# Strassen's seven products for the v, u and g products of a gMLP layer

## The chip, the core and the metric

The kernel runs on one core of one Trainium2 chip. The metric is the device time of one execution in microseconds (us). TensorE (PE) multiplies, VectorE (DVE), ScalarE (ACT) and GpSimd (POOL) do the rest, and SyncE (SP) and GpSimd issue the transfers between DRAM and the core's on-chip memory.

## The reference, cut to what matters

One sequence of 2048 tokens with 1024 features goes through one gMLP layer (A) and one attention layer (B), in float32. The change is in layer A's input product.

```python
def gmlp_mixer(h, w_in, ln_g, ln_b, ws, bs, w_out):
    z = h @ w_in                          # 1024 -> 3 * 2048
    u, v, g = jnp.split(z, 3, axis=-1)
    v = layer_norm(v, ln_g, ln_b)
    ...
    sv = jnp.einsum('gts,bcsgd->bctgd', wsm, v) + bs.T[:, :, None]   # per chunk of 128 tokens, 16 groups
    y = u * sv * jax.nn.silu(g)
    return y @ w_out

h = x + gmlp_mixer(rms_norm(x, a_norm_g), ...)
# then swa_mixer (attention in a window of 128 tokens) and a last rms_norm
```

## The kernel before

The tokens are worked in four blocks of 512 (`TB`), first all four through layer A, then all four through layer B. To keep float32's precision, every dense operand is split into a high and a low part (`split`: ACT casts the high part, DVE or POOL subtracts it for the low part), and each product is three matrix products (`mm3`): high by high, high by low, low by high.

A block of layer A has three stages. `vphase` makes v with tokens on partitions: 4 column blocks of 512, and for each of them 4 weight slabs, with 24 products of 512 columns a slab. Then come 16 column groups j of 128: `proj` makes u and then g for each, one slab and 24 products of 512 columns each, and `gate(j)` follows a product later: four small products with the spatial weights on TensorE, two steps on DVE, a multiply on POOL (L381), and a `split` on ACT and DVE. Last, `outproj_a` makes the output product with 16 slabs and adds x.

Weights come as slabs of 128x1024 (512 KB). `fetch` loads one from the SP queue into one of two raw buffers (`w_raw`), and `split` turns it into one of four buffers `w` (high and low part); `weights` hands out the next and keeps three fetched or under way. The raw buffer is free again after DVE's subtraction, and the `w` buffer after the last product that reads it.

Other work is put between the products by a count of half slabs: `half` advances the count, and `after(n, f)` calls f some halves later. In this way come the norm of x (`sumsq_step`, `rnorm`, `xn_step`), the next block's sums of squares, and `prescale`, which multiplies layer B's weights by a gain on POOL, splits them and stores them in DRAM, in 18 jobs. The framework's scheduler then sets the final order on each engine's queue, and each engine works its queue strictly in that order. On-chip tiles of 128x512 (`slot`) come from one pool of 39; there are eight PSUM banks (`bank`).

Of the kernel before, what the change touches and what calls it, by code (L numbers as in the profile page):

```python
# [18 lines left out]
P = 128  # L19
# [7 lines left out]
NJ = AW // P  # L27
NQ = 4
# [9 lines left out]
GEN_BUFS = 39  # L38
# [6 lines left out]
GATE_ENG = 'V'  # L45
FIRST_W = (0, 2, 5)
PIECES = "k00 k01 q00 q01 g00 q10 q11 g01 q20 q21 g10 q30 q31 g11 g20 g21 g30 g31".split()
# [9 lines left out]
def trunk(ctx: ExitStack, tc: tile.TileContext, xT, wv, wug, wao, wkv, wqg, wbo, wsT, bs, gains, lngb,  # L57
# [6 lines left out]
    xpool = ctx.enter_context(tc.tile_pool(name="xpool", bufs=8))  # L64
    gen = ctx.enter_context(tc.tile_pool(name="gen", bufs=GEN_BUFS))
    sm = ctx.enter_context(tc.tile_pool(name="sm", bufs=6))
    psum = ctx.enter_context(tc.tile_pool(name="psum", bufs=8, space=bass.MemoryType.PSUM))
# [5 lines left out]
    wkvD, wqgD = wbD[:2], wbD[2:]  # L73

    chain = [None]

    def load(dst, src):
        """A load from the sync queue; while chain is set, in the order of the program."""
        if chain[0] is None:
            nc.sync.dma_start(dst, src)  # L80
            return
        with tc.issue_after(chain[0]):
            chain[0] = nc.sync.dma_start(dst, src).ins
# [103 lines left out]
    def by_token(mean, n):  # L187
        """(mean + eps)^-1/2 of n * 128 tokens, from mean on every partition to [P, n] by token."""
# [10 lines left out]
    def rnorm(acc, done, wait=RN1, wait2=RN2, on_r4=None):  # L199
        """Calls done(r) with r on every partition, some half pieces later; on_r4 gets it by token."""  # L200
# [42 lines left out]

    def hn_steps(b, hh, hl):
        """The steps that make hn of a block, one per feature tile."""
        box = []

        def step(k):
            if not box:
                r = slot()  # L250
                nc.sync.dma_start(r, rD[b])
                box.append(r)
            raw = slot()
            nc.sync.dma_start(raw, hD[b][k])
            V.tensor_tensor(raw, raw, box[0], ALU.mult)
            h = xpool.tile([P, TB], F32R, name="x_hi")
            l = xpool.tile([P, TB], F32R, name="x_lo")
            split(h, l, raw)
            hh.append(h)
            hl.append(l)  # L260
# [3 lines left out]
    # ================= layer A =================  # L264
    with ExitStack() as actx:
        ac = actx.enter_context(tc.tile_pool(name="ac", bufs=1))
        pre = actx.enter_context(tc.tile_pool(name="pre", bufs=1))
        wraw[0] = pre

        ws_sb = ac.tile([P, NJ, P], F32, name="ws_sb")  # L270
        lngb_sb = ac.tile([P, 2, NJ], F32, name="lngb_sb")
        ln_g, ln_b = lngb_sb[:, 0, :], lngb_sb[:, 1, :]
        cb = ac.tile([P, NJ, P], F32, name="cb")

        def load_consts():
            load(ws_sb, wsT)
            G.affine_select(out=ws_sb, in_=ws_sb, pattern=[[0, NJ], [1, P]], base=0, channel_multiplier=-1,
                            compare_op=ALU.is_ge, fill=0.0)
            load(lngb_sb, lngb)
            load(cb.rearrange("p j t -> p (j t)"), bs.partition_broadcast(P))  # L280
            chain[0] = None

# [15 lines left out]
        def xn_step(k, xr, r, xh, xl):  # L298
            V.scalar_tensor_tensor(xr, xr, a_g[:, k:k + 1], r, ALU.mult, ALU.mult)
            h = xpool.tile([P, TB], F32R, name="x_hi")  # L300
            l = xpool.tile([P, TB], F32R, name="x_lo")
            split(h, l, xr)
            xh.append(h)
            xl.append(l)

        def make_cb():
            for q in range(4):
                ps = bank()
                PE.matmul(ps, ones, ws_sb[:, 4 * q:4 * q + 4, :], start=True, stop=True)
                for i in range(4):  # L310
                    j = 4 * q + i
                    V.scalar_tensor_tensor(cb[:, j, :], ps[:, i * P:(i + 1) * P], ln_b[:, j:j + 1], cb[:, j, :],
                                           ALU.mult, ALU.add)
# [12 lines left out]
        def prescale_job(src, dst, g, nk):  # L326
            w = pre.tile([P, 1024], F32, name="pw")
# [3 lines left out]
            hl = pre.tile([P, 2048], F32R, name="phl")  # L331
# [3 lines left out]
        def vphase(xh, xl, r4=None):  # L335
            vt = [[None] * 4 for _ in range(TT)]
            st = [sm.tile([P, 4, 6], F32, name="bst", bufs=8) for _ in range(TT)]
            for cbk in range(4):
# [12 lines left out]
                for t in range(TT):  # L351
                    v = slot()
                    if r4 is None:
                        A.copy(v, pss[t])
                    else:
                        A.activation(v, pss[t], AF.Copy, scale=r4[0][:, t:t + 1])
                    V.bn_stats(st[t][:, cbk, :], v)
                    vt[t][cbk] = v
            for t in range(TT):
# [5 lines left out]
                G.tensor_tensor(rs, ve, neghalf, ALU.pow)  # L365
                for cbk in range(4):
# [3 lines left out]
        def gate(j, vt, psu, psg, yh, yl):  # L370
            sg = slot()
            A.activation(sg, psg, AF.Silu)
            psm = bank()
            for t in range(TT):
                PE.matmul(psm[:, t * P:(t + 1) * P], vt[t][j // 4][:, (j % 4) * P:(j % 4 + 1) * P], ws_sb[:, j, :],  # L375
                          start=True, stop=True)
            sv = slot()
            V.scalar_tensor_tensor(sv.rearrange("p (c t) -> p c t", c=TT), psm.rearrange("p (c t) -> p c t", c=TT),
                                   ln_g[:, j:j + 1], cb[:, j, None, :].broadcast_to([P, TT, P]), ALU.mult, ALU.add)
            V.tensor_tensor(sv, psu, sv, ALU.mult)  # L380
            last[0] = G.tensor_tensor(sv, sv, sg, ALU.mult).ins  # L381
            h, l = slot(F32R), slot(F32R)
            split(h, l, sv)
            yh.append(h)
            yl.append(l)
# [21 lines left out]
        xh, xl, r4 = [], [], []  # L407
# [9 lines left out]
        def first_xn(r):  # L417
            for k in range(KD):
                after(2 * k, lambda k=k: xn_step(k, raws[k], r, xh, xl))
# [11 lines left out]
        after(18, make_cb)  # L431
        for b in range(NB):
            vt = vphase(xh, xl) if b else vphase(fh, fl, r4)
            yh, yl = [], []
            pend = None
            for j in range(NJ):
                psu = proj(xh, xl)
                if pend:
                    gate(*pend)
                psg = proj(xh, xl)  # L440
                pend = (j, vt, psu, psg, yh, yl)
                if j % 2 == 1:
                    prescale()
                if b + 1 < NB and j == 6:
                    for k, f in enumerate(stat_steps(b + 1, got.append)):
                        after(2 * k, f)
            gate(*pend)
            if b + 1 < NB:
                xh, xl = [], []
                r = got.pop()  # L450
                for k in range(KD):
                    after(2 * k + 1, lambda k=k, b=b, r=r, xh=xh, xl=xl: xn_step(k, load_x(b + 1, k), r, xh, xl))
# [8 lines left out]
    # ================= layer B =================  # L461
# [16 lines left out]
    def rope(src, nh, t0, nt, tab):  # L478
        """src [P, nt, nh, 64] rotated, as [P, nt * nh * 64] of a new slot."""
# [12 lines left out]
    def natural(ps, t2, t, w2, hh, hl):  # L492
        """ps[:, t2, :] = hn[t].T @ W for 256 columns."""
# [73 lines left out]
    def g_piece(i, sg, hh, hl):  # L567
        A.copy(sg[:, i, :], proj(hh, hl))
# [306 lines left out]
```

## Time and profile before

| | us |
|---|---|
| median of 3 runs | 2268.8 (2268.7 to 2269.88) |
| span of the profiled execution | 2266.6 |
| TensorE busy, by the profile's model | 2239.9 |
| DVE, ACT, POOL busy | 1240.9, 889.2, 619.3 |

The profile describes one execution, from its first to its last instruction. Of that execution only the span is given, 2.2 us under the median of the three runs. Line numbers (L113) are those of the kernel before. In groups, a number after x is a count, and "idle before" names what ended the wait. In the rows for one tile, three numbers with strokes are the shortest, the median and the longest duration in ns.

### The profile page before, as it was taken

Reading aid. Unit: us, or ns where it says so; the run is one execution under the profiler, and the core shown is the slowest. Engines: PE = TensorE matmul, PEld = TensorE weight load, DVE = VectorE, ACT = ScalarE, POOL = GpSimd, SP = SyncE. Lnnn points to the kernel's source line nnn. Section 1 sums busy time; section 2 is a strip of 40 time slices with the busy share of each in tenths; the row PEclk is TensorE's granted clock in tenths of the full one; section 3 lists DMA queues with packets and bytes.
Section 4 is the critical chain, followed back from the end, with each engine's and each line's share of the span. In section 5 each row is a group of like instructions: output and inputs, shape, how many; then the busy total and the mean of one; then the engine's idle time right before and its main releaser. Section 6 shows DMA issues by size and latency. Waiting matters only on the chain.

```text
span 2266.6 us, 31103 instructions
## 1 busy us (share of the span) xinstructions
PE 2239.9 (99%) x11868; PEld 1922.9 (85%) x11868; DVE 1240.9 (55%) x2145; ACT 889.2 (39%) x1781; POOL 619.3 (27%) x667
## 2 busy tenths in 40 slices
PE   8999999999999999999999999999999999999997
PEld 7888888888888888888888888899889889989987
DVE  6543553354453344345335335258957867895785
ACT  5323332323332322323222223135725744662573
POOL 2034322023532003311101111225513622551461
PEclk9999999999999999999999999999999999999999
DMA  6245453335455324325332224543364255336322
GB/s 214 85 154 189 163 204 126 100 120 176 151 202 178 105 93 149 122 92 177 121 107 89 89 93 149 179 174 114 101 219 155 94 195 186 112 121 235 120 94 93
DMA packets 90005, 319.59 MB, mean 141 GB/s; under 512 B 10625, under 2 KB 12929, under 8 KB 78081
## 3 DMA queue, kind: packets, MB, share of 16 engines
q1 hardware_dynamic: 71424, 204.35, 26.8%
q0 software_dynamic: 18432, 113.26, 14.5%
q8 instruction: 94, 1.54, 0.3%
q14 instruction: 55, 0.44, 0.1%
HBM read 280.86 MB, written 36.70 MB: 140 GB/s over the span
## 4 chain that ended last, share of the span: by engine, by line
PE 85%; DVE 6%; issue 3%; ACT 2%; DMA 2%; POOL 2%; POOLq 0%; SPq 0%; DVEq 0%; ACTq 0%
PE ps L116 26%; PE ps L117 26%; PE ps L118 25%; PE ps L375 2%; PE ps L641 2%; PE ps L588 1%; PE ps L619 1%; PE ps L589 1%; DVE w L113 1%; PE ps L560 1%; DVE x_lo L113 1%; DMA s<-h 1%; ACT w L112 1%; DMA s<-in_xT 1%; POOL s L381 0%
## 5 line engine op out<-in xcount | busy, mean ns | idle before, releaser
L113 DVE TENSOR_TENSOR w<-w_raw,w 128x1024 fp32r<-128x1024 f32 x288 | 378.4, 1314 | 369.5 <-ACT w L112 369.1
L116 PE MATMUL ps<-x_hi,w 128*128 128x512 f32 x1280 | 506.3, 396 | 0.0
L117 PE MATMUL ps<-x_lo,w 128*128 128x512 f32 x1280 | 499.0, 390 | 0.0
L118 PE MATMUL ps<-x_hi,w 128*128 128x512 f32 x1280 | 498.6, 390 | 0.0
L112 ACT CAST w<-w_raw 128x1024 fp32r<-128x1024 f32 x288 | 301.0, 1046 | 499.2 <-PE ps L118 375.8
L116 PE MATMUL ps<-w,x_hi 128*128 128x256 f32 (+1 forms) x1024 | 332.1, 324 | 0.0
L118 PE MATMUL ps<-w,x_lo 128*128 128x256 f32 (+1 forms) x1024 | 330.5, 323 | 0.0
L117 PE MATMUL ps<-w,x_hi 128*128 128x256 f32 (+1 forms) x1024 | 330.4, 323 | 0.0
L116 PE MATMUL ps<-s,w 128*128 128x512 f32 (+1 forms) x800 | 305.2, 383 | 4.5 <-ACT s L112 4.5
L117 PE MATMUL ps<-s,w 128*128 128x512 f32 (+1 forms) x800 | 305.0, 381 | 0.1
L118 PE MATMUL ps<-s,w 128*128 128x512 f32 (+1 forms) x800 | 304.4, 381 | 0.0
L118 PEld LDWEIGHTS ps<-x_hi,w 128*128 128x128 f32 x1280 | 240.3, 188 | 50.5
L116 PEld LDWEIGHTS ps<-x_hi,w 128*128 128x128 f32 x1280 | 240.7, 188 | 46.0
L117 PEld LDWEIGHTS ps<-x_lo,w 128*128 128x128 f32 x1280 | 240.8, 188 | 45.7
L627 POOL TENSOR_SCALAR_AFFINE_SELECT s<-s 128x512 fp32r<-128x512 f32 x256 | 184.8, 749 | 101.7 <-ACT s L621 69.3
L117 PEld LDWEIGHTS ps<-w,x_hi 128*128 128x128 f32 x1024 | 194.7, 190 | 15.6
L116 PEld LDWEIGHTS ps<-w,x_hi 128*128 128x128 f32 x1024 | 194.6, 190 | 15.5
L118 PEld LDWEIGHTS ps<-w,x_lo 128*128 128x128 f32 x1024 | 194.7, 190 | 15.1
L381 POOL TENSOR_TENSOR s<-s 128x512 f32<-128x512 f32 x64 | 82.2, 1284 | 396.0 <-DVE s L380 335.6
L116 PEld LDWEIGHTS ps<-s,w 128*128 128x128 f32 x800 | 150.2, 188 | 33.8 <-ACT s L112 6.0
L117 PEld LDWEIGHTS ps<-s,w 128*128 128x128 f32 x800 | 150.5, 188 | 29.2 <-DVE s L113 1.4
L118 PEld LDWEIGHTS ps<-s,w 128*128 128x128 f32 x800 | 150.4, 188 | 28.5
(145 smaller groups left out, 2871.5 us busy)
## 6 DMA issues: line engine op xcount, KB each, us to landing
w<-wb POOLq DMA_DIRECT2D x72, 1024.0 KB, 5.4
w_raw<-in_wug SPq DMA_DIRECT2D x128, 512.0 KB, 3.7
w_raw<-in_wv SPq DMA_DIRECT2D x64, 512.0 KB, 3.7
w_raw<-in_wao SPq DMA_DIRECT2D x64, 512.0 KB, 3.8
s<-in_xT SPq DMA_DIRECT2D x88, 256.0 KB, 4.4
wb<-phl POOLq DMA_DIRECT2D x18, 1024.0 KB, 5.2
w_raw<-in_wbo SPq DMA_DIRECT2D x32, 512.0 KB, 3.8
s<-h SPq DMA_DIRECT2D x64, 256.0 KB, 4.7
```

Of the source, the lines that this page charges most:

```text
L112: A.copy(hi, src)
L113: (lo_eng or V).tensor_tensor(lo, src, hi.bitcast(F32), ALU.subtract)
L116: PE.matmul(ps, ah, bh, start=first, stop=False)
L117: PE.matmul(ps, ah, bl, start=False, stop=False)
L118: PE.matmul(ps, al, bh, start=False, stop=last)
L375: PE.matmul(psm[:, t * P:(t + 1) * P], vt[t][j // 4][:, (j % 4) * P:(j % 4 + 1) * P], ws_sb[:, j, :], start=True, stop=True)
L381: last[0] = G.tensor_tensor(sv, sv, sg, ALU.mult).ins
L560: PE.transpose(pst[:, h * P:(h + 1) * P], sts[t2][:, h].rearrange("p s d -> p (s d)"), ident_r)
L588: PE.matmul(o, lq, kst[:, kv, 0, band, :], start=True, stop=False)
L589: PE.matmul(o, lq, kst[:, kv, 1, band, :], start=False, stop=True)
L627: G.affine_select(out=y.rearrange("p (h q) -> p h q", h=4), in_=x.rearrange("p (h q) -> p h q", h=4), pattern=[[0, 4], [sign, P]], base=ba ...
L641: PE.matmul(po[:, par * 256:(par + 1) * 256], w, x[:, par * 256:(par + 1) * 256], start=n == 0, stop=n == 3)
```

## The change

The v product of blocks 1 to 3, and the u and g product of all blocks, are computed as 2 x 2 block products with seven instead of eight sub-products. The quarters are: features 0 to 511 and 512 to 1023 of x by the first and last 256 tokens of a block, and the same features of the weights by two column halves (u and g, or two column blocks of v). Three sub-products take plain quarters ("11", "12", "22") and four take sums of quarters ("s1" to "s4"). Some results are kept in PSUM and accumulated on, and are copied out in between (`keep_one`).

For u and g, two groups j form a pair; eight pairs make a block. A pair takes seven slabs, one for each sub-product, with 24 products of 256 columns each, and then the gates of both j, which are issued after the next pair's "12". For v, each half of the columns takes seven sub-products of two slabs, with 12 products of 512 columns a slab. Layer A now has 388 slabs instead of 256.

The weights' sums are formed once, in block 0, by POOL: `weight_sums` loads four quarters, makes four sums and stores them in DRAM, in 12 jobs, one every four halves in the program; later they are loaded as slabs. The sums of x are formed by DVE in `xn_step`. `prescale` moves from all blocks to blocks 1 to 3. The spatial weights and biases, which stayed on chip, go to DRAM once and are loaded for each pair (`wc`). There are 41 slots. In layer B the gate's Silu and multiply are done in halves.

```diff
+STEPS = ("11", "12", "s2", "s1", "s3", "s4", "22")
-        order += [wv[i] for i in range(16)] + [wug[i] for i in range(32)] + [wao[i] for i in range(16)]
+        if b == 0:
+            order += [wv[i] for i in range(16)]
+        else:
+            for g in range(2):
...
+        for p in range(NP):
+            for n in STEPS:
+                order.append(wuq[p, PLAIN.index(n)] if n in PLAIN[:2] else wuq[p, 3] if n == "22" else
+                             suD[p][int(n[1]) - 1])
...
-        def xn_step(k, xr, r, xh, xl):
+        def xn_step(k, x1, x2, r, xs):
+            for x, n in ((x1, k), (x2, k + 4)):
+                V.scalar_tensor_tensor(x, x, a_g[:, n:n + 1], r, ALU.mult, ALU.mult)
+            ta, tb = slot(), slot()
+            a11, a12, a21, a22 = x1[:, :TH], x1[:, TH:], x2[:, :TH], x2[:, TH:]
+            V.tensor_tensor(ta[:, :TH], a12, a11, ALU.subtract)
+            V.tensor_tensor(ta[:, TH:], a22, ta[:, :TH], ALU.subtract)
+            V.tensor_tensor(tb[:, :TH], a22, a12, ALU.subtract)
+            V.tensor_tensor(tb[:, TH:], a21, ta[:, TH:], ALU.subtract)
+            h, l = xpair(xlast if k == 3 else xpool)
+            for i, z in enumerate((x2, ta, tb, x1[:, :TH])):
+                zs = slice(i * TB, i * TB + z.shape[-1])
+                split(h[:, zs], l[:, zs], z)
+            xs.append((h, l))
...
+        def weight_sums(pool):
+            src, dst = sum_jobs.pop(0)
+            a11, a12, a21, a22 = (pool.tile([P, 1024], F32, name=f"qa{i}") for i in range(4))
+            for t, i in ((a21, 2), (a22, 3), (a11, 0), (a12, 1)):
+                G.dma_start(t, src[i])
+            G.tensor_tensor(a22, a21, a22, ALU.add)
+            G.tensor_tensor(a21, a11, a21, ALU.subtract)
+            G.tensor_tensor(a11, a22, a11, ALU.subtract)
+            G.tensor_tensor(a12, a12, a11, ALU.subtract)
+            for i, t in enumerate((a22, a11, a21, a12)):
+                G.dma_start(dst[i], t)
...
+        def chain_of(product, width, done):
+            a = [bank() for _ in range(width)]
+            keep = lambda banks: [keep_one(ps) for ps in banks]
+            def keep_one(ps):
+                t = slot()
+                A.copy(t, ps)
+                return t
+            product(a, "11", True)
+            p1 = keep(a)
+            c = [bank() for _ in range(width)]
+            product(c, "12", True)
+            done(11, c, p1)
+            product(a, "s2", False)
+            u2 = keep(a)
+            c = [bank() for _ in range(width)]
+            product(c, "s1", True)
+            p5 = keep(c)
+            product(a, "s3", False)
+            done(22, a, p5)
+            product(c, "s4", False)
+            done(12, c, u2)
+            product(a, "22", False)
+            done(21, a, None)
...
+        def ug_pair(p, xs, pend):
+            us, sgs = [slot(), slot()], [slot(), slot()]
+            def product(banks, n, first):
+                wh, wl = weights()
+                xo = slice(XOF[n] * TH, (XOF[n] + 1) * TH)
+                for jj in range(2):
+                    for k in range(4):
+                        cs = slice((4 * jj + k) * P, (4 * jj + k + 1) * P)
+                        mm3c(banks[0][:, jj * TH:(jj + 1) * TH], wh[:, cs], wl[:, cs], xs[k][0][:, xo], xs[k][1][:, xo],
+                             first and jj == 0 and k == 0)
+                half()
+                if n == "12" and pend:
+                    gate(*pend)
...
+        for i in range(len(sum_jobs)):
+            after(2 + 4 * i, lambda: weight_sums(sums))
         for b in range(NB):
-            vt = vphase(xh, xl) if b else vphase(fh, fl, r4)
+            vt = vphase_fast(xs) if b else vphase(fh, fl, r4)
...
+            for p in range(NP):
+                pend = (p, vt, *ug_pair(p, xs, pend), yh, yl)
+                if b:
+                    prescale()
```

**POOL in block 0.** Before, the queue goes from the layer norm's four steps (L365) to the first gate multiply (L381), and then takes a prescale job.

```order
L277 AFFINE_SELECT ws_sb_156<-ws_sb_156 128x2048
L365 TENSOR_TENSOR rs_871<-ve_869,neghalf_144 128x1
L365 TENSOR_TENSOR rs_881<-ve_879,neghalf_144 128x1
L365 TENSOR_TENSOR rs_891<-ve_889,neghalf_144 128x1
L365 TENSOR_TENSOR rs_901<-ve_899,neghalf_144 128x1
L381 TENSOR_TENSOR s_1004<-s_1004,s_997 128x512
```

Now, with the first gate multiply as L542: `su7` is the last store target of the eighth job, and the loads of `qa` from `in_wv` open the ninth and the tenth.

```order
L380 DMA su7_3_160<-qa1_1064 128x1024
L374 DMA qa2_1228<-in_wv 128x1024
L374 DMA qa3_1229<-in_wv 128x1024
L374 DMA qa0_1226<-in_wv 128x1024
L374 DMA qa1_1227<-in_wv 128x1024
L375 TENSOR_TENSOR qa3_1229<-qa2_1228,qa3_1229 128x1024
L542 TENSOR_TENSOR s_1490<-s_1490,s_1162 128x512
L376 TENSOR_TENSOR qa2_1228<-qa0_1226,qa2_1228 128x1024
```

The first gate's multiply stands behind eight whole jobs and the ninth's first add; the second stands in the same way behind the tenth's first add, the third and fourth behind the eleventh's and the twelfth's.

**ACT in block 0, at pairs 1 and 2.** Before, a gate's cast (L112 from `s_1004`) stands between two Silus (L372) and weight casts.

```order
L372 ACTIVATE s_997<-ps_942 128x512
L112 CAST w_1012<-w_raw_1013 128x1024
L112 CAST w_1049<-w_raw_1050 128x1024
L112 CAST s_1008<-s_1004 128x512
L372 ACTIVATE s_1079<-ps_1017 128x512
```

Now (L123 is the cast, L446 the copy of `keep_one`): `s_1494` and `s_1507` are the casts of pair 0's two gates, `w_1655` is pair 2's "12", `w_1707` its "s2", and the two copies are pair 1's after s2 and s1.

```order
L123 CAST w_1624<-w_raw_1625 128x1024
L123 CAST s_1494<-s_1490 128x512
L123 CAST w_1655<-w_raw_1656 128x1024
L123 CAST w_1707<-w_raw_1708 128x1024
L123 CAST s_1507<-s_1503 128x512
L446 COPY s_1558<-ps_1421 128x512
L446 COPY s_1590<-ps_1560 128x512
```

The casts of pair 0's gates came ahead of the copies that pair 1's s3 and s4 wait for.

**TensorE in block 3, where one pair passes into the next.** Rows of the change: `ps_12440` with `w_12350` is the end of s1, `w_12504` is the next pair's "11" (it stands in the buffer of `w_12350`), and `w_12409` is s3.

```order
L135 MATMUL ps_12440<-x_hi_10387,w_12350 128x256
L133 MATMUL ps_12570<-x_hi_10124,w_12504 128x256
L134 MATMUL ps_12570<-x_lo_10125,w_12504 128x256
...
L135 MATMUL ps_12570<-x_hi_10124,w_12504 128x256
L133 MATMUL ps_12317<-x_hi_10124,w_12409 128x256
L134 MATMUL ps_12317<-x_lo_10125,w_12409 128x256
```

And ACT at the same place: `w_12504`'s cast, a gate's cast, and the copies after s2 and s1.

```order
L123 CAST w_12472<-w_raw_12473 128x1024
L123 CAST w_12504<-w_raw_12505 128x1024
L123 CAST s_12403<-s_12399 128x512
L446 COPY s_12438<-ps_12317 128x512
L446 COPY s_12470<-ps_12440 128x512
```

Fifteen products of the next pair's first slab moved ahead of s3, and on ACT that slab's cast stands ahead of the copy that s3 waits for.

More of the change, by code (lines that the diff above doesn't have):

```diff
@@ L242, in proj, with xpair @@
         return ps
+    def xpair(pool=xpool):
+        return [pool.tile([P, 7 * TH], F32R, name=n) for n in ("x_hi", "x_lo")]
     def hn_steps(b, hh, hl):
@@ L255, in step @@
             V.tensor_tensor(raw, raw, box[0], ALU.mult)
[L256 to L257 removed]
+            if k % 3 == 0:
+                box[1:] = xpair()
+            h, l = (z[:, (k % 3) * TB:(k % 3 + 1) * TB] for z in box[1:])
             split(h, l, raw)
@@ L417, in first_xn @@
         def first_xn(r):
-            for k in range(KD):
-                after(2 * k, lambda k=k: xn_step(k, raws[k], r, xh, xl))
+            for k in range(4):
+                after(4 * k, lambda k=k: xn_step(k, raws[k], raws[k + 4], r, xs))
         box = [None]
```

206 lines of the change are left out of this document (136 added, 70 removed).

## The prediction

> **What bounds the kernel now.** I read the page first, for who is busy and what the chain runs on.
>
> ```profile
> span 2266.6 us, 31103 instructions
> ...
> PE 2239.9 (99%) x11868; PEld 1922.9 (85%) x11868; DVE 1240.9 (55%) x2145; ACT 889.2 (39%) x1781; POOL 619.3 (27%) x667
> ...
> PE 85%; DVE 6%; issue 3%; ACT 2%; DMA 2%; POOL 2%; POOLq 0%; SPq 0%; DVEq 0%; ACTq 0%
> ```
>
> TensorE carries the chain. Its busy time is modelled, so I took its rate from the timeline, as the distance between starts: the first and last of 15 products with 512 columns, then of 42 with 256.
>
> ```profile
> 1467.74 0.39 PE L116 MATMUL ps<-s,w 128*128 128x512 f32 x1
> ...
> 1470.92 0.39 PE L118 MATMUL ps<-s,w 128*128 128x512 f32 x1
> 1471.14 0.28 PE L116 MATMUL ps<-w,x_hi 128*128 128x256 f32 x1
> ...
> 1476.06 0.28 PE L118 MATMUL ps<-w,x_lo 128*128 128x256 f32 x1
> ```
>
> That is 3.18/14 = 0.227 us and 4.92/41 = 0.120 us: 256 columns cost 6% over half of 512. Then the chain in order of time, at the gate's small products (its pieces mark where each j ends), and one whole block from gate to gate.
>
> ```profile
> 117.61 0.89 PE ps L375 x8
> ...
> 289.95 0.89 PE ps L375 x8
> ...
> 847.36 0.89 PE ps L375 x8
> 859.15 0.89 PE ps L375 x8
> ```
> ```profile
> 847.36:1212.00 364.64, 364.64 (x1674) 304.19 (x1674) 155.06 (x190) 111.21 (x142) 65.91 (x55) 1.00 0.38 125
> ```
>
> Two j take 23.58 us, which is 96 x 0.227 + 2 x 0.89; TensorE never stops in a gMLP block (columns: us, TensorE, weight loads, DVE, ACT, POOL busy, clock, DMA share, GB/s). The page's span is 2266.6, 2.2 below the runs' median of 2268.8; I add differences to the median.
>
> **What TensorE saves.** u and g: 768 products of 512 columns a block become 1344 of 256, 174.3 to 161.3 us, -13.0, four times -52. v: 384 become 336, 87.2 to 76.3, -10.9, three times -33. If all else hid, 2268.8 - 85 = 2184.
>
> **The weight stream.** Each Strassen product eats a weight slab of its own. In the v part a slab lasts 12 x 0.227 = 2.72 us, in u/g 24 x 0.120 = 2.88; now 5.44. Both kernels have two raw buffers: a load waits for the DVE subtraction that empties one.
>
> ```profile
> L112 ACT CAST w<-w_raw x288: 1031/1047/1069, 5.7 to 2233.4; 128x1024 fp32r<-128x1024 f32 x144
> L113 DVE TENSOR_TENSOR w<-w_raw,w x288: 1193/1226/2586, 6.7 to 2234.5; 128x1024 fp32r<-128x1024 f32 x144
> ...
> DMA to landing us min/median/max: 3.3/3.7/7.2
> ```
> ```profile
> SPq L80 <- DVE w L113: 1783.5, 272, 139.0
> ```
>
> One turn of a buffer is 3.7 + 1.05 + 1.23 + 0.1 for hand-overs = 6.1 us, a slab every 3.03 us at best. So v in blocks 1 to 3 becomes bound by the stream: 28 x 3.03 = 85 instead of 76.3. The slabs ahead save about 6 us, DVE's four pairs of adds and statistics per half (0.69 each) stand between the subtractions and cost about as much: 85.
>
> ```profile
> L354 ACT COPY s<-ps 128x512 f32<-128x512 f32 x48 | 28.2, 588 | 31.4 <-PE ps L118 31.4
> L646 ACT COPY o<-ps 64x256 f32<-64x256 f32 x64 | 23.6, 369 | 20.0 <-PE ps L641 18.1
> L112 ACT CAST s<-s 128x512 fp32r<-128x512 f32 x75 | 46.6, 621 | 282.0 <-POOL s L381 257.3 <-POOL s L184 22.4 <-DVE s L184 2.3
> L378 DVE SCALAR_TENSOR_TENSOR s<-ps,lngb_sb,cb 128x512 f32<-128x512 f32 x64 | 48.0, 750 | 176.6 <-PE ps L375 176.6
> L380 DVE TENSOR_TENSOR s<-ps,s 128x512 f32<-128x512 f32 x64 | 43.7, 683 | 0.2
> L357 DVE BATCH_NORM_STATS2 bst<-s 128x6 f32<-128x512 f32 x64 | 43.9, 690 | 17.5 <-ACT s L354 15.7 <-ACT s L356 1.8
> L367 DVE TENSOR_SCALAR s<-s,mv,rs 128x512 f32<-128x512 f32 x64 | 30.3, 538 | 0.9 <-POOL rs L365 0.7
> ```
>
> At the end of v twelve of the sixteen normalizing steps (0.54 each, 6.5 us) stand on DVE ahead of the subtraction for pair 0's s1; hidden now, they are then a stall of about 6. So v: 85 + 6 against 87.2, +4 a block (ends -8, all hidden but a few us, and +15).
>
> **A pair in steady state.** The order puts, on TensorE, 15 (or 2) products of the next pair's "11" between s1 and s3. There are four w buffers, and that next slab goes into the one that s1 frees. So its cast can only start when s1 ends, and ACT has the copies that s3 and s4 wait for behind it. Clock from the start of s2: s1 ends at 5.76; cast to 6.9, subtraction to 8.1; two products need the cast alone, 13 wait for the subtraction, 1.56; s3 at 9.7, not 7.56. Then s3, s4, 22, the rest of 11, 12 and two gates, 14.4: 24.1 at least, already over 23.58. The raw loads add to it. With E the start of s3: 12's slab is subtracted at E+5.2 (after s3, DVE's add 0.7, cast, subtraction); its raw buffer's next load (next s1) lands at E+9.0, its cast waits for the Silus of 22 (E+9.4) and its subtraction ends at E+11.75; the load of s4's slab lands at E+15.5, 1.1 us after the next pair's start, is cast and subtracted by 3.4; the next load lands at 7.1, cast 8.1, subtraction 9.4, 13 products, s3 at 11.0. So E = 11.0, a pair 25.4: TensorE 21.94 and 3.4 of waiting. A block's u/g is 161.3 + 14.2 + 7 x 3.4 = 199 against 188.5: +11 (ends +3 and +20). Blocks 1 to 3: 3 x (4 + 11) = +45.
>
> **Block 0: GpSimd.** It now forms the sums: 12 jobs, each 4 loads, 4 adds, 4 stores of 512 KB, with one set of buffers, in one queue with the gate's multiplies.
>
> ```profile
> L381 POOL TENSOR_TENSOR s<-s x64: 1271/1286/1293, 121.2 to 1387.0; 128x512 f32<-128x512 f32 x64
> ```
> ```profile
> L184 POOL TENSOR_TENSOR s<-s x56: 1262/1622/2155, 18.1 to 1473.0; 128x512 f32<-128x512 f32 x56
> ```
> ```profile
> L365 POOL TENSOR_TENSOR rs<-ve,neghalf x16: 552/572/1238, 99.4 to 1199.6; 128x1 f32<-128x1 f32 x16
> ```
> ```profile
> 31.50 0.49 PE L207 MATMUL ps<-s,inv_r 128*128 128x512 f32 x1
> ```
> ```profile
> L330 POOL TENSOR_TENSOR pw<-pw,g_sb x18: 1883/1886/2002, 127.1 to 880.6; 128x1024 f32<-128x1024 f32 x18
> ...
> L113 POOL TENSOR_TENSOR phl<-pw,phl x18: 2387/2400/2409, 130.2 to 883.7; 128x1024 fp32r<-128x1024 f32 x18
> L328 POOL DMA_DIRECT2D pw<-in_wqg x16: 591/596/640, 169.5 to 875.7; - x16
> ...
> DMA to landing us min/median/max: 3.8/4.6/6.7
> ```
> ```profile
> wb<-phl POOLq DMA_DIRECT2D x18, 1024.0 KB, 5.2
> ...
> h<-s POOLq DMA_DIRECT2D x32, 256.0 KB, 2.3
> ```
>
> An add of 128x1024 is 2.5 (between 2.40 and 2 x 1.286), an issue 0.6, a load 4.6, a store 3.3 (between 2.3 and 5.2 by size). From a job's last add: two stores issued, 1.2; two loads issued, the second landing at 6.4; the last two wait for the stores (3.3, 3.9) and are issued by 4.5; four adds with two store issues between, 11.2: 17.6. With the weight stream beside it I take 18.5 (ends 15, adds as L330's, and 22, landings of 6.7). Job 0 ends near 19, its loads landing near 8. Job 1 has seven additions and a subtraction of the first norm between its adds (L184, 1.6 each), so that norm, used at 31.5 us now (L207), comes near 46, and TensorE waits some 15 us there, inside the time that follows. Job 2 ends near 68, job 7 near 163 (with 2.3 for four of L365). The first gate multiply stands behind job 8's first add, the next three behind job 9's, 10's and 11's: they end at 174, 194, 214 and 233 us. Now the first is at 121 (L381). On ACT the casts of these gates stand ahead of weight casts and of the copies that s3 of pairs 1 and 2 wait for. So TensorE cannot start pair 2's s3 before 235 (a cast and a copy after 233), then five products to 249, 31 more (89), five pairs' gates and a norm's four products (10), five waits (16): u/g ends near 364. Before it ended at 291 (the chain's row at 289.95): +73 (ends +35 and +115).
>
> The Trainium skill, "DMA: Bandwidth & Descriptors", Anatomy of one DMA, gives 2.0 us and bytes/436e3 for a load from this queue: 3.2 for 512 KB, where the trace has 4.6. By it a job is 1.4 shorter and the sum some 15 lower; the trace's figure is used.
>
> **Prescaling (blocks 1 to 3).** 18 jobs that lay in the first three blocks; 16 now fall beside pairs that have no slack.
>
> ```profile
> 130.19 2.40 POOL L113 TENSOR_TENSOR phl<-pw,phl 128x1024 fp32r<-128x1024 f32 x1 [1.16 <-ACT phl L112]
> ...
> 131.09 2.58 DVE L113 TENSOR_TENSOR w<-w_raw,w 128x1024 fp32r<-128x1024 f32 x1
> ```
>
> A subtraction that meets a GpSimd operation lasts until that ends and its own 1.23 more. Such a job costs the loop about 1.35 for one subtraction, up to 1.6 for the cast of phl ahead of 12's cast, and slower landings: 3 a pair (ends 1 and 4.5), +48.
>
> The Trainium skill, "SBUF — State Buffer", Who interferes with whom, calls this an exclusive lock, for a DVE operation with two SBUF inputs against a GpSimd read, and says that whoever starts second waits. The trace agrees for DVE (2.58); GpSimd's 2387 to 2409 ns show no wait. If the 48 adds waited 0.3 each, block 0 would be 14 longer; that stays out of the sum.
>
> **Layer B.** ACT gets 16 more table loads (50 against 34), since the gate's Silu comes in halves.
>
> ```profile
> L652 ACT ACT_TABLE_LOAD  x16: 1283/1283/1283, 1528.1 to 2204.1; - x16
> ```
> ```profile
> 1666.00:1861.00 195.00, 192.65 (x1269) 174.46 (x1268) 150.35 (x331) 104.62 (x294) 76.29 (x100) 1.00 0.44 154
> ```
>
> 5 us a block on an engine busy 105 of 195: +3 in all (ends 0 and 20). The heavier xn_step (sums of x) lies beside the output product, whose slabs last 5.44: nothing, unless that cover goes. The gate's constants now come by a load a pair, issued two pairs ahead: nothing. Some eight more slots are in use late in u/g, of 41 instead of 39; that can only add, and is left to the range.
>
> **Sum.** 73 + 45 + 48 + 3 = 169; 2268.8 + 169 = 2438.
>
> **Rivals.** (A) Faster: TensorE stays the bound, 2184 to 2260. It decides where a slab comes every 2.7 us and the gates' multiplies do not wait for the sums; a raw turn of 6.1 us for two buffers, and the queue's order, speak against it. (B) GpSimd's work is mostly hidden: block 0 and prescaling at their lower ends (35, and 1 x 16), v at -8 and u/g at +11 (three times +3): 2268.8 + 35 + 16 + 9 + 3 = 2332; it decides at jobs of 15 us. (C) Transfers crowd: 4 MB a job in 18.5 us is 227 GB/s, and weights come on top, against 125 GB/s in the block above. At landings of 6.7 a slab takes (6.7 + 2.4)/2 = 4.5: prescaled pairs 31.5, so 6 x 16 = 96, and block 0 at +115: 2268.8 + 115 + 45 + 96 + 3 = 2528. That the products shrink less than said is no rival: their number stands in the code.
>
> **How the numbers follow.** The forecast 0.73, B 0.12, C 0.10, A 0.05. The range leaves out A, half of B and half of C: 2340 to 2530. Within 0.2% (4.5 us, about what a measurement here can tell) lies only a mix of A and B, 0.02; faster 0.05; slower 0.93.
>
> **What would show it.** Right: block 0's u/g ends near 364, with ACT's gate casts waiting for POOL some 100 us in all; pairs of 25 us in block 3, with TensorE waiting for the ACT cast and the DVE subtraction of a next "11"; v near 85. Wrong: pairs of 22 us, or a job much off 18.5.

## The result, and the profile after

| | before | after |
|---|---|---|
| median of the runs, us | 2268.9 | 2567.7 (2565.4 to 2578.5) |
| ratio to before | | 1.132 (95% interval 1.130 to 1.135) |
| span of the profiled execution, us | 2266.6 | 2576.4 |

The kernel became 13% slower: +299 us, where +169 was forecast with a range that ended at +261. The profiled execution of after is the longest of the four; its span is 310 above that of before, and the 310 is what the rows below divide.

First the page of after: span, busy time, and the row of the granted TensorE clock in 40 slices, which read 9 throughout before.

```profile
span 2576.4 us, 37018 instructions
...
PE 2260.8 (88%) x14028; PEld 2035.5 (79%) x14028; DVE 1582.1 (61%) x2585; ACT 1115.3 (43%) x2137; POOL 814.5 (32%) x814
...
PEclk8987889998889999888999989999899999999999
```

TensorE's modelled busy time rose by 21 us although its products shrank, and the share fell from 99 to 88%. The granted clock is down to 0.8 or 0.7 in 13 of the 40 slices. Both are read by stage: two tables of windows (columns: us, TensorE, weight loads, DVE, ACT, POOL busy, clock, DMA share, GB/s), cut where the stages end. Of before: block 0's v, block 0's u/g, block 1's v and u/g, block 3's u/g, and the rest from block 3's output product on.

```profile
0.00:101.30 101.30, 94.49 (x397) 75.74 (x398) 59.31 (x90) 45.89 (x62) 16.40 (x17) 1.00 0.47 161
101.30:290.60 189.30, 189.30 (x900) 158.93 (x900) 88.92 (x107) 64.04 (x83) 71.33 (x56) 1.00 0.47 160
...
377.70:465.90 88.20, 88.20 (x390) 72.96 (x390) 34.28 (x43) 27.01 (x34) 5.78 (x6) 1.00 0.31 102
465.90:655.30 189.40, 189.40 (x901) 158.88 (x900) 88.32 (x106) 62.43 (x82) 71.23 (x56) 1.00 0.48 159
1195.70:1384.00 188.30, 188.30 (x896) 158.22 (x896) 76.21 (x99) 51.15 (x65) 21.50 (x18) 1.00 0.27 90
1384.00:2266.60 882.60, 862.75 (x5563) 776.68 (x5561) 630.35 (x1386) 447.44 (x1217) 320.78 (x419) 1.00 0.43 148
```

The same stages of after:

```profile
0.00:136.60 136.60, 100.74 (x396) 78.65 (x397) 93.83 (x107) 45.98 (x66) 96.21 (x85) 0.91 0.79 293
136.60:417.80 281.20, 201.26 (x1478) 196.91 (x1477) 161.58 (x176) 97.67 (x140) 136.46 (x106) 0.83 0.61 218
...
504.80:583.90 79.10, 79.10 (x342) 63.62 (x342) 50.75 (x60) 36.10 (x44) 6.14 (x5) 1.00 0.54 173
583.90:833.20 249.30, 196.58 (x1477) 191.85 (x1476) 134.02 (x173) 101.82 (x144) 75.50 (x55) 0.87 0.53 177
...
1418.20:1648.40 230.20, 193.03 (x1483) 188.79 (x1481) 127.89 (x169) 90.99 (x128) 28.77 (x22) 0.90 0.46 151
1648.40:2576.40 928.00, 875.43 (x5553) 782.75 (x5551) 627.30 (x1403) 474.53 (x1251) 316.71 (x420) 0.97 0.42 141
```

| stage | before | after | difference | forecast |
|---|---|---|---|---|
| block 0, to the end of u/g | 290.6 | 417.8 | +127 | +73 |
| v, blocks 1 to 3 | 3 x 88 | 79.1, 79.1, 78.6 | -27 | +12 |
| u/g, blocks 1 to 3 | 190, 189, 188 | 249, 249, 230 | +161 | 33 + 48 |
| block 3's output product and layer B | 882.6 | 928.0 | +45 | +3 |

The output products of blocks 0 to 2 make up the rest, +3. So v did better than forecast, and the other three lines did worse.

What a u/g pair of block 3 looks like, on TensorE's timeline (start, duration, operation, idle time before it): the last product of s1, the first products of the next "11", and products a little later.

```profile
1577.04 0.28 PE L135 MATMUL ps<-x_hi,w 128*128 128x256 f32 x1
1580.22 0.39 PE L133 MATMUL ps<-x_hi,w 128*128 128x256 f32 x1 [2.90 <-ACT w L123]
...
1581.48 0.39 PE L135 MATMUL ps<-x_hi,w 128*128 128x256 f32 x1 [0.76 <-DVE w L124]
...
1583.16 0.41 PE L134 MATMUL ps<-x_lo,w 128*128 128x256 f32 x1
1583.37 0.41 PE L135 MATMUL ps<-x_hi,w 128*128 128x256 f32 x1
...
1585.93 0.28 PE L135 MATMUL ps<-x_hi,w 128*128 128x256 f32 x1
1586.05 0.28 PE L133 MATMUL ps<-x_hi,w 128*128 128x256 f32 x1
```

The two waits are the forecast ones: for the cast and for the subtraction of the next "11", 2.90 + 0.76 = 3.7 us where 3.4 was forecast. The cast starts 1.8 us after s1 has ended, since its slab's load landed only then: the turn of the raw buffers came last. The new thing is behind the waits. From 1582.5 to 1585.9, for 3.4 us, products of 256 columns start 0.21 us apart instead of 0.12: the clock is halved, with nothing to wait for. That costs the pair another 1.5 us (16 starts, 0.095 more each). Counted over all starts of the four u/g stages (intervals between 1.3 and 2 times the usual one), the excess is 22, 19, 17 and 16 us, 74 in all; the same count finds 5 in the kernel before.

The Trainium skill, "TensorE: Matmul & The Clock Gate", Part 1, says that TensorE's clock is halved after an idle window of about 3.4 us, that the windows run freely, and that it takes such a window of work to come back. The trace agrees in the length of the slow stretch, 3.4 us. It differs in that the wait here, 2.90, is shorter than such a window; the stretch begins 2.3 us after the wait has ended. The granted clock, read in steps of 3.41 us, shows where it changes:

```profile
1575.68:1579.09 3.41, 1.64 (x15) 1.43 (x13) 2.63 (x4) 0.42 (x1) 0.64 (x1) 1.00 0.68 226
1579.09:1582.51 3.42, 1.53 (x10) 1.33 (x11) 2.31 (x4) 2.54 (x4) 0.63 (x1) 1.00 0.54 172
1582.51:1585.92 3.41, 3.41 (x18) 3.41 (x17) 0.19 (x1) 0.00 (x0) 0.00 (x0) 0.50 0.42 144
```

In the first step TensorE idled for 1.8 us and the clock stayed; in the second it idled for 1.9, and the third ran at half.

Block 0, on GpSimd's timeline: the first add of the ninth and the twelfth job, each with the gate multiply behind it. Then the DMA view (size, median us to landing), of the whole run, and of weight slabs in block 0's v, in after and in before.

```profile
197.80 2.35 POOL L375 TENSOR_TENSOR qa<-qa,qa 128x1024 f32<-128x1024 f32 x1 [4.25 <-DMA qa<-in_wv]
200.10 2.25 POOL L542 TENSOR_TENSOR s<-s 128x512 f32<-128x512 f32 x1
...
265.43 2.39 POOL L375 TENSOR_TENSOR qa<-qa,qa 128x1024 f32<-128x1024 f32 x1 [1.87 <-DMA qa<-in_wv]
267.79 1.26 POOL L542 TENSOR_TENSOR s<-s 128x512 f32<-128x512 f32 x1
```
```profile
w_raw<-sv SPq DMA_DIRECT2D x48, 512.0 KB, 3.2
...
qa<-in_wuq POOLq DMA_DIRECT2D x32, 512.0 KB, 6.9
```
```profile
w_raw<-in_wv SPq DMA_DIRECT2D x16, 512.0 KB, 6.1
```
```profile
w_raw<-in_wv SPq DMA_DIRECT2D x16, 512.0 KB, 3.9
```

The first gate multiply ends at 202 and the fourth at 269, where 174 and 233 were forecast: the jobs come every 22.5 us, (265.4 - 197.8)/3, where the forecast has 19.7 (a job of 18.5 and a gate multiply). Most of the difference is a load's landing after 6.9 us, not 4.6. While the jobs run, weight slabs land late as well: after 6.1 us in v, and after 5.2 to 5.7 in u/g up to 280 us; behind that after 3.3 to 3.8.

At 270.2 us pair 2's s3 starts right behind the fourth gate's cast (269.1) and a copy (269.6), on the path that the prediction names. But TensorE waited only 2.0 us for them. Of its 58 us of waits in u/g up to there, 7.7 ended with a copy behind a gate's cast. The two longest were 12.6, for an add on DVE behind the layer norm's steps (L435, three of which lasted 2.7 to 3.0 us instead of 0.54 while GpSimd worked), and 13.4, for a slab whose raw buffer came free late, since the two loads before it had taken 8 us.

### The profile page after: what moved, and what is told of

Same layout as the page of the kernel before. It is cut to its first block, busy times and chain, and to the rows that moved or that the text cites. A ratio compares the mean times of both kernels' runs of the same rounds, so it can differ in the third digit from the quotient of the medians.

```text
span 2576.4 us, 37018 instructions
## 1 busy us (share of the span) xinstructions
PE 2260.8 (88%) x14028; PEld 2035.5 (79%) x14028; DVE 1582.1 (61%) x2585; ACT 1115.3 (43%) x2137; POOL 814.5 (32%) x814
## 5 line engine op out<-in xcount | busy, mean ns | idle before, releaser
L124 DVE TENSOR_TENSOR w<-w_raw,w 128x1024 fp32r<-128x1024 f32 x420 | 558.4, 1330 | 467.9 <-ACT w L123 462.2
L123 ACT CAST w<-w_raw 128x1024 fp32r<-128x1024 f32 x420 | 440.1, 1048 | 686.4 <-DMA w_raw<-su 141.7
L133 PE MATMUL ps<-x_hi,w 128*128 128x256 f32 x1792 | 543.2, 303 | 187.0 <-ACT w L123 145.2
L135 PE MATMUL ps<-x_hi,w 128*128 128x256 f32 x1792 | 533.4, 299 | 35.8 <-DVE w L124 35.5
L134 PE MATMUL ps<-x_lo,w 128*128 128x256 f32 x1792 | 533.1, 298 | 0.0
L133 PEld LDWEIGHTS ps<-x_hi,w 128*128 128x128 f32 x1792 | 373.3, 208 | 197.2 <-ACT w L123 151.6
L135 PEld LDWEIGHTS ps<-x_hi,w 128*128 128x128 f32 x1792 | 370.5, 207 | 42.8 <-DVE w L124 42.8
L134 PEld LDWEIGHTS ps<-x_lo,w 128*128 128x128 f32 x1792 | 374.0, 209 | 0.3
L542 POOL TENSOR_TENSOR s<-s 128x512 f32<-128x512 f32 x64 | 103.2, 1612 | 474.8 <-DVE s L541 390.4
L127 PE MATMUL ps<-w,x_hi 128*128 128x256 f32 x640 | 181.9, 284 | 8.8 <-ACT s L718 6.7
L128 PE MATMUL ps<-w,x_hi 128*128 128x256 f32 x640 | 180.0, 281 | 0.0
L129 PE MATMUL ps<-w,x_lo 128*128 128x256 f32 x640 | 179.8, 281 | 0.0
L134 PE MATMUL ps<-w,x_hi 128*128 128x512 f32 x336 | 132.6, 395 | 0.0
L135 PE MATMUL ps<-w,x_lo 128*128 128x512 f32 x336 | 132.5, 394 | 0.0
L133 PE MATMUL ps<-w,x_hi 128*128 128x512 f32 x336 | 132.3, 394 | 0.0
```

Source lines behind the costliest of these rows:

```text
L123: A.copy(hi, src)
L124: (lo_eng or V).tensor_tensor(lo, src, hi.bitcast(F32), ALU.subtract)
L127: PE.matmul(ps, ah, bh, start=first, stop=False)
L128: PE.matmul(ps, ah, bl, start=False, stop=False)
L129: PE.matmul(ps, al, bh, start=False, stop=last)
L133: PE.matmul(ps, ah, bh, start=first, stop=False, skip_group_check=True)
```

## Experiments

Each was compared with the kernel before on the same chip.

**Layer B's part alone.** The kernel before, with the gate of layer B as in the changed one:

```diff
-        A.activation(sg, sg, AF.Silu)
-        YE = {'V': V, 'G': G}[GATE_ENG]
-        YE.tensor_tensor(o, o, sg, ALU.mult)
         for i in range(2):
+            A.activation(sg[i], sg[i], AF.Silu)
+            V.tensor_tensor(o[:, i, :], o[:, i, :], sg[i], ALU.mult)
```

> The kernel before with one part of the change alone: layer B's gate in halves (a Silu and a multiply for each half, the halves in slots). Theory: this part alone sets another order on the queues in layer B, with stalls of TensorE of 2 to 4.4 us, three a block, and half clock behind them; then the whole +45 of layer B appears here: 2269 + 45 = 2314 (2305 to 2320). Rival 1: only the 16 more table loads count, 1.3 us each, mostly hidden: 2269 to 2275. Rival 2: layer B is slow in the changed kernel because layer A hands its data over late; then this kernel stays at 2269.

2321.5 us, ratio 1.023 (1.022 to 1.025): +53, a little over the expected range. So the part that was priced at 3 costs by itself all that layer B lost in the changed kernel (45), with layer A as before. On TensorE's and DVE's queues the order in layer B is now the changed kernel's, row for row. The waits of TensorE in layer B (us in total, times, longest):

```profile
PE ps L116 <- DVE s L623: 15.4, 4, 4.0
PE ps L116 <- ACT s L112: 7.5, 3, 3.1
PE ps L116 <- ACT s L552: 6.7, 3, 2.2
```

One such wait in the changed kernel, in order of time, from the last score product to the product that waits:

```profile
2265.13 0.28 PE L756 MATMUL ps<-kst,s 128*128 128x256 f32 x1
...
2266.88 0.42 DVE L655 TENSOR_TENSOR s<-s 128x256 f32<-128x256 f32 x1
...
2267.37 0.71 ACT L718 CAST s<-s 128x256 fp32r<-128x256 f32 x2 [4.65 <-issue]
...
2267.99 0.59 ACT L788 ACTIVATE s<-ps 128x512 fp32r<-128x512 f32 x1
...
2268.67 0.69 DVE L789 TENSOR_TENSOR s<-ps,s 128x512 f32<-128x512 f32 x1
2269.28 0.41 DVE L763 TENSOR_REDUCE mx<-ps 128x2 f32<-128x256 f32 x1
2269.41 0.80 PE L127 MATMUL ps<-x_hi,w 128*128 128x512 f32 x1 [4.00 <-DVE s L789]
```

ACT stood idle for 4.65 us at a cast (L718) that needs DVE's rotation (L655). Behind it stood the copy of the transposed probabilities (L788), then DVE's subtraction (L789), and TensorE's product was released by that. The 16 table loads of 1.28 us are 20 us in all, less than half of the 53, even if none were hidden; the order on the queues is what brings such waits, three a block. In all TensorE waits 43.5 us in layer B, against 11.8 in the kernel before, and half clock, counted as above, adds about 19: 51 of the 53. The edit also puts the two halves into tiles of the slot pool, where they had shared a tile of their own; which of its two parts sets the new order was not tried.

**Strassen for v alone**, u, g and layer B as before. Block 0's sums are formed in eight half jobs of 512 columns on GpSimd, in between the gates:

```diff
-            vt = vphase(xh, xl) if b else vphase(fh, fl, r4)
+            vt = vphase_fast(xh, xl, xt) if b else vphase(fh, fl, r4)
...
-                if j % 2 == 1:
-                    prescale()
+                if j % 2 == 1:
+                    prescale() if b else weight_sums(sums)
```

> Strassen for v in blocks 1 to 3 alone; u, g and layer B as before; the sums of v's weights are formed in eight half jobs beside block 0's u/g. Theory: the v stage takes 79 us in place of 88 in three blocks, its slabs keep up with TensorE, and eight half jobs find room between the gate multiplies: 2269 - 27 = 2242 (2236 to 2250). Rival, as predicted before the run: v is bound by the two raw buffers (85) and the layer norm's steps stall pair 0 (6): 2269 + 12 = 2281; and the sums may delay the gates of block 0, up to 20 more.

2256.2 us, ratio 0.995 (0.993 to 0.996), less gain than expected. The v stages took 80 to 81 us against 88, but the output product of block 0 lost 8. One row of TensorE's waits around it:

```profile
PE ps L123 <- ACT s L119: 5.1, 1, 5.1
```

**The same, with the half jobs earlier:**

```diff
-                if j % 2 == 1:
-                    prescale() if b else weight_sums(sums)
+                if b == 0:
+                    if j in (1, 2, 3, 5, 7, 9, 11, 13):
+                        weight_sums(sums)
+                elif j % 2 == 1:
+                    prescale()
```

> As e2 (Strassen for v alone), with the eight half jobs of weight sums done by j = 13 in place of 15, so that none stands near the last gate of block 0. In e2 the output product of block 0 waited 5.1 us for the cast of the last gate, and half clock cost 2.1 behind it. Theory: that stall was the last half job's on GpSimd: 2256 - 8 = 2248 (2245 to 2251). Rival: it is the opening of the pools after block 0, which the move doesn't touch: 2254 to 2258.

2246.1 us, ratio 0.990 (0.988 to 0.991): as the theory has it, the stall is gone, and with it the half clock behind it. Block 1's v and u/g:

```profile
378.30:459.00 80.70, 80.34 (x345) 64.16 (x344) 51.86 (x61) 35.98 (x45) 6.13 (x5) 1.00 0.52 170
459.00:647.60 188.60, 188.60 (x896) 158.37 (x895) 91.38 (x111) 64.62 (x84) 71.77 (x57) 1.00 0.55 178
```

**And with a third raw buffer** (`NRAW = [3]` for layer A, one `wc` in place of two):

> As e8 (Strassen for v alone, 2246), with three raw buffers in layer A in place of two (and one buffer for a pair's gate constants in place of two). In e8 the v stage lasted 80 to 81 us, of which 78.5 was TensorE's work, and waits for DVE's subtraction of a slab 1 to 2. Theory: the raw buffers' turn is what is left: 2 us a block less, 2246 - 5 = 2241. Rival: TensorE's own rate (0.231 us a product there, against 0.227) is the bound: 2245 to 2248.

2242.8 us, ratio 0.989 (0.987 to 0.990); the v stages' products span 78.2 to 78.3 us against 79.6 to 81.5. That is what the theory says of the stage, but the intervals of the two ratios overlap. This is the fastest version measured, 26 us under before.

**No weight sums:**

```diff
-        for i in range(len(sum_jobs)):
-            after(2 + 4 * i, lambda: weight_sums(sums))
+        sum_jobs.clear()
...
-                             suD[p][int(n[1]) - 1])
+                             wuq[p, int(n[1]) - 1])
```

> The changed kernel without the forming of weight sums: GpSimd's 12 jobs are left out, and where a sum's slab was loaded a plain quarter of the weights is loaded (so these products work on other data). Theory: GpSimd's jobs hold up block 0; its v falls from 137 to about 103 us and its u/g from 281 to 230, as in block 3: 2568 - 34 - 51 = 2483 (2470 to 2500); blocks 1 to 3 unchanged. Rival: block 0's u/g is held by the weight stream and the clock like the rest, and the jobs are hidden behind that: only the v part, 34, and at most 10 more: 2524 to 2540.

2473.6 us, ratio 1.091 (1.089 to 1.094): 94 less than the changed kernel. Its windows for block 0's v, block 0's u/g and block 1's u/g:

```profile
0.00:101.00 101.00, 94.04 (x398) 75.88 (x399) 67.41 (x114) 49.05 (x71) 17.16 (x20) 1.00 0.54 178
101.00:317.60 216.60, 186.10 (x1476) 182.28 (x1475) 126.59 (x170) 94.16 (x136) 36.27 (x26) 0.93 0.48 152
...
485.30:733.50 248.20, 196.60 (x1477) 191.88 (x1476) 134.15 (x174) 102.05 (x144) 75.59 (x55) 0.88 0.55 179
```

Block 0's v is back at 101, its u/g at 217 (from 281), and block 1 is unchanged. So by the two profiles the jobs cost 36 in v and 65 in u/g, and even without them u/g is slower than the 189 of before. This run takes away the jobs' hold on GpSimd's queue and their transfers at once, so it does not part the two.

**Buffers**, three variants of the kernel without weight sums: three raw buffers; five `w` buffers and four slabs ahead, with 38 slots; both. One run each.

> The kernel without the forming of weight sums (as e3: plain quarters in place of the sums), and with three raw buffers in layer A in place of two. Compared with e3 in block 3, whose pairs without prescaling lasted 27.0 us there (25.1 to 27.6). Theory of the prediction: the slab of the next 11 is held by two things, the turn of the raw buffers and the w buffer that s1 frees; a third raw buffer brings its load early, its cast then starts as s1 ends: s3 starts at 9.7 in place of 11, the wait is 2.3, too short for most half-clock windows: pairs of 24 to 25.5, block 3's u/g about 205 to 215 in place of 230. Rival: the w buffers alone decide (ACT's casts wait for TensorE 6 us with slabs that have landed): 26.5 to 27.5, no change. Rival 2: transfers crowd, more loads at a time land later: 27 to 30.

> As e3, with five w buffers in place of four and four slabs fetched ahead in place of three (38 slots in place of 41, one raw buffer in layer B, so layer B isn't compared). Theory of the prediction: the next 11 no longer stands in the buffer that s1 frees, so its cast isn't tied to the end of s1; the two raw buffers give a slab in 3.03 us, 21.2 a pair, under TensorE's 21.6: pairs of 22 to 24 in block 3 without prescaling, u/g 180 to 200. Rival: the raw buffers' turn decides, with its casts behind ACT's copies: 26 to 27.5.

> As e3, with three raw buffers and five w buffers, four slabs fetched ahead (38 slots, one raw buffer in layer B). Theory: both bounds are lifted, TensorE is the bound: pairs of 21.6 to 22.5 without prescaling, u/g of block 3 176 to 185, granted clock 1.0; a pair then beats the 23.58 of the kernel before. Rival: ACT's and DVE's queues (copies, casts, the gate) or the transfers hold it at 24 or more.

The window of three pairs of block 3 without prescaling, in the kernel without sums, then with three raw, with five `w`, with both:

```profile
1443.80:1525.20 81.40, 69.19 (x555) 67.97 (x555) 44.37 (x54) 33.39 (x49) 7.69 (x6) 0.94 0.47 146
```
```profile
1390.90:1465.50 74.60, 67.43 (x555) 65.50 (x554) 43.32 (x55) 33.04 (x48) 10.18 (x6) 0.98 0.50 159
```
```profile
1445.80:1519.70 73.90, 65.33 (x553) 63.91 (x553) 45.17 (x54) 33.47 (x48) 11.36 (x6) 1.00 0.51 161
```
```profile
1402.10:1473.00 70.90, 66.08 (x554) 64.75 (x553) 42.71 (x54) 32.68 (x49) 10.30 (x6) 1.00 0.54 167
```

A pair takes 27.1, 24.9, 24.6 and 23.6 us. The clock returns to full as the waits get short. Both the raw turn and the `w` buffer held the next "11", as the prediction said, and either one lifted takes away most. Three raw buffers did what was expected; five `w` buffers were expected to reach 24 or less and did not. With both the pair stops at 23.6, not at the 21.6 to 22.5 expected, and so does not beat the 23.58 of before. These waits are left there, in the three pairs:

```profile
PE ps L136 <- DVE w L125: 3.2, 3, 1.1
PE ps L134 <- ACT s L447: 1.6, 3, 0.5
```

DVE's subtraction of a slab and ACT's copy of a kept result still come late. In these windows slabs landed after a median of 3.5, 4.3, 3.7 and 3.9 us, too little for the rival of crowded transfers.

Block 3's whole u/g took 230, 204, 212 and 193 us; 188 before. The whole kernels took 2473.6, 2412.6, 2471.5 and 2425.0. With five `w` buffers and 38 slots each v stage lengthened from some 80 us to between 96 and 100, with one wait of 11 to 14 us for a norm in it; why the norm came late there was not looked into.

**A filler in the place of the wait**, in the changed kernel, ahead of s3 of each pair:

```diff
+            filler(width)                # 30 x matmul(ps[:, :256], ones_r, x_hi) into a bank of its own
             product(a, "s3", False)
```

> The changed kernel with 30 more products of 256 columns in each u/g pair, ahead of s3, into a PSUM bank that nothing reads; with them the order has next to no product of the next 11 ahead of s3. It adds 32 x 30 x 0.12 = 115 us of work to TensorE. Theory: TensorE's clock is halved for 3.4 us behind each wait of about 3 us; kept busy it stays at full clock, the filler (3.5 us) stands in the place of the wait, and the half-clock excess of the u/g stages (22 + 19 + 17 + 16 = 74 us) mostly goes: 2568 - 60 = 2508 (2490 to 2540), with the granted clock of a u/g stage near 1.0. Rival: the clock is no cause of its own, the pair is set by when slabs arrive, and a filler only adds: 2568 to 2680.

2590.4 us, ratio 1.141 (1.140 to 1.143): 23 slower than the changed kernel, so as a whole the rival's number, and the expected gain is missed. Of 115 us that were added, some 90 vanished. The windows tell where: two pairs of block 3 beside prescaling and the next four, cut at the fillers, and then three of the four in the changed kernel.

```profile
1484.00:1546.30 62.30, 55.56 (x431) 55.13 (x430) 30.59 (x39) 24.21 (x34) 12.28 (x8) 0.89 0.57 186
1546.30:1650.50 104.20, 99.97 (x859) 99.15 (x858) 58.30 (x73) 44.45 (x64) 15.32 (x8) 1.00 0.50 152
```
```profile
1541.70:1625.00 83.30, 71.32 (x554) 70.00 (x553) 44.58 (x54) 33.38 (x49) 7.69 (x6) 0.92 0.43 143
```

The four pairs without prescaling take 26.1 us at full clock, in the changed kernel 27.8 at 0.92, with 30 products less each. The two beside prescaling take 31.1: behind the filler s3 waits another 3.4 us for ACT (for a weight cast in one, for a copy in the other), and the clock falls again. The filler also moved the next "11" behind the pair, so the difference of 1.7 us is not the clock's alone. That the clock follows the waits is what the rows show in every kernel here; it was not isolated from them.

**Prescaling without arithmetic.** The multiply, ACT's cast and GpSimd's subtraction are left out, the transfers stay:

```diff
-            G.tensor_tensor(w3, w3, g[:, :, None].broadcast_to([P, nk, 1024 // nk]), ALU.mult)
...
-            split(hl[:, :1024], hl[:, 1024:], w, G)
+            G.dma_start(hl[:, :1024], src)
+            G.dma_start(hl[:, 1024:], src)
```

> The changed kernel, in which prescaling only moves data: the two loads and the store of each job stay on GpSimd's queue (one load more), its multiply, the cast on ACT and the subtraction on GpSimd are left out, so layer B works on other weights. Theory of the prediction: GpSimd's two long operations, and ACT's cast that waits for them, cost 3 us a pair in 16 pairs: 2568 - 48 = 2520 (2510 to 2535), the pairs of blocks 1 and 2 near 27 to 28 in place of 29 to 33. Rival: the prescaled pairs are long because their transfers crowd the weight loads, or because of the next block's sums of squares that stand there too: 2560 to 2575.

2528.7 us, ratio 1.115 (1.113 to 1.117): 39 less than the changed kernel, 2.4 for each of 16 pairs. The arithmetic carries 39 of the 48 that were forecast for prescaling; what its transfers cost was not tried.

## Why the prediction was wrong, by its steps

- **Direction and place** were right: GpSimd's queue in block 0, the next "11" in a steady pair, prescaled pairs. The size was not: 2438 against 2568, outside the range.
- **The weight stream and v** (+4 a block with the layer norm): mis-sized. With landings of 3.2 us (`w_raw<-sv`) the turn is 5.6, a slab every 2.8, and TensorE's 12 products take 12 x 0.231 = 2.77. So v took 79, near TensorE's rate, where 85 was forecast. The stall of 6 behind the layer norm did come, in u/g's first pair: twelve L435 steps stood for 5.56 us ahead of a subtraction, and TensorE waited 3.6 for it.

```profile
591.25 5.56 DVE L435 TENSOR_SCALAR s<-s,mv,rs 128x512 f32<-128x512 f32 x12
596.73 1.22 DVE L124 TENSOR_TENSOR w<-w_raw,w 128x1024 fp32r<-128x1024 f32 x1
```

- **A pair in steady state** (25.4 us): the wait was nearly right, 3.7 in the pair shown and 4.0 a pair over three, against 3.4, and so was its cause, which the buffer variants show. The steps came as forecast: counted from the start of s2 (1571.5) the load landed at 7.5 (forecast 7.1), the cast ended at 8.7 (8.1) and the subtraction at 9.9 (9.4). The step that failed is the sum behind it: it took TensorE's rate as given, 21.94 a pair, where the profile has 23.8 (71.32/3), and the pair was 27.8. Half clock behind a wait had no term, and it is 74 us over the four u/g stages. In blocks 1 to 3 it is 52, while the waits, 144, were not far from the 3 x 24 + 48 of the sum. The view of before could not show it, since TensorE hardly waited there; the page of the Trainium skill named above would have given a rival, and was not weighed.
- **Block 0** (+73): the path was right in its outline, from the jobs to the fourth gate to pair 2's s3; the job was mis-sized, 22.5 us with the gate multiply for 19.7. By the fourth gate that is 36, and from there to the end of u/g another 19 (148 us for 129). But the sign that was named for it, ACT's gate casts waiting for GpSimd some 100 us, did not come: they waited 23. TensorE was nearly as late by slabs that landed late and by DVE. So the gates alone are not shown to be the cause; the jobs are, with 94 us by the run without them. The late norm (L236) cost TensorE 15.3, as forecast, late slabs and subtractions another 14.8 in v; by pair 2's s3 these had been absorbed, as the prediction says of the norm.
- **Prescaling** (+48): right within 9 for the arithmetic. (In the rows shown for it, the subtraction ends 1.1 us behind GpSimd's, not 1.23.)
- **Layer B** (+3, ends 0 and 20): the step that failed outright. It priced the table loads and took the order of the other instructions as unchanged. It was +45, and the experiment with that part alone gives +53, by waits of TensorE that the new order brings.
- **The rivals**: C came nearest, at 2528, in part by luck. Transfers did crowd in block 0, where weight slabs landed after 5.2 to 6.1 us; but beside prescaling, where C has 96 us, u/g's slabs landed after 3.5 to 4.0. None had the clock or layer B.

The parts that were tried by themselves: sums 94, layer B 53, prescaling 39, v -23. If they add up, which was not tried, the u/g product with its waits and half clock is left with about 299 - 94 - 53 - 39 + 23 = 136.

## What to carry to other kernels

Fewer products pay only where each slab is handed over in time. v, with a slab every 2.8 us, gained up to 26 us of 2269. u/g, with one every 2.9 us, lost its gain: the first slab of the next pair stood ahead of products that did not need it, and even with more buffers a pair took as long as before. Price a wait of TensorE with the half clock behind it: 224 us of waits in the four u/g stages brought 74 more. And an edit that looks local, such as an activation in halves, is priced by the order that it leaves on the queues around it, not by its own instructions.

## What the runs showed of the hardware

- In the traces here the granted clock changes only at the edges of windows of 3.41 us, and half clock lasts one or several whole windows. What counts is TensorE's idle time within a window, about half of it, and not the length of one wait. In the changed kernel 50 windows at full clock were followed by half clock, and TensorE had idled for 1.6 us or more in each; 602 were followed by full clock, with 1.9 or less. Two waits of 1.2 us close together were enough once, 1.8 us of idling in the window up to 1524.5 us. Full clock came back only behind windows with 0.2 us of idling or less.
- In the windows of block 3 without prescaling shown above, the granted clock was 0.98 to 1.00 where no wait was over 1.6 us, and 0.92 to 0.94 where the longest was 3.8 to 4.0.
- Beside the jobs, which load and store 4 MB each, 512 KB landed late on both queues of block 0: after 6.9 and 7.4 us for GpSimd's loads, 5.2 to 6.1 for SP's weight slabs. Over the whole run SP's slabs landed after 3.2 to 3.8.
- A 512-column product in the v form with seven sub-products starts every 0.231 us, against 0.227 before. What makes the difference was not tried.
